# Where the normed state lies in SBUF: 32 KB of matmul operands move to a pool of their own, at another address modulo 512 bytes

## The chip, the core and the metric

The kernel runs on one core of a Trainium2 chip. TensorE (PE, with PEld for its weight loads), VectorE (DVE), ScalarE (ACT), GpSimd (POOL) and the DMA queue that SyncE (SP) issues work side by side and meet at semaphores. The metric is the device time of one execution in microseconds (us), lower is better, as the median of several runs.

## The reference, cut to what matters

The program is a two-layer diffusion backbone over 256 latent tokens and 256 context tokens of width 1024, everything in float32. Layer 0 mixes tokens by a grouped 2-D Fourier transform, layer 1 by retention. Each layer puts a half-step SwiGLU feed-forward block (FFN, inner width 2816) before and after its mixer.

```python
def _modnorm(h, g, shift, scale):
    return _rmsnorm(h, g) * (1.0 + scale) + shift

def _ffn_half(h, g, shift, scale, gate, w_in, w_out):
    a, b = jnp.split(_modnorm(h, g, shift, scale) @ w_in, 2, axis=-1)
    return h + 0.5 * gate * ((jax.nn.silu(a) * b) @ w_out)
...
for i in range(DEPTH):
    h = _ffn_half(h, norm_g[i, 0], m[:, 0], m[:, 1], m[:, 2], ffn_w_in[i, 0], ffn_w_out[i, 0])
    u = _modnorm(h, norm_g[i, 1], m[:, 3], m[:, 4])
    ...
    h = h + m[:, 5] * y
    h = _ffn_half(h, norm_g[i, 2], m[:, 6], m[:, 7], m[:, 8], ffn_w_in[i, 1], ffn_w_out[i, 1])
```

The normed state u is what every first matrix of a block multiplies: `w_in` of the FFN, the queries, keys and gates of retention, and the channel transform of the Fourier mixer.

## The kernel before

The state is held transposed: 128 features on the partitions, tokens along the free dimension, latent tokens in columns 0 to 255 and context tokens in 256 to 511. A product in float32 is made of three float32r matmuls: each operand is split into a high part (tag `h`, or pool `hip`) and a low part (tag `l`, or `lop`), and `mm3` (lines 132 to 135) issues high times high (L133), high weights times low state (L134) and low weights times high state (L135), each with a weight load of its own of 128x128.

`new_u` (line 272) hands out the normed state: 16 tiles `uh0`, `ul0` ... `uh7`, `ul7` of 128 x 512 float32r, 2048 bytes of each partition. It is called seven times, and since the tags repeat and the pool has one buffer for a tag, all seven users share the same 16 places. In a trace all of these tiles are called `u`.

Weights come in through `unit` (line 114): 512 KB loads into `raw` (pool `rawp`, 7 buffers), a copy to `hi` by ACT (L121) and a difference to `lo` by DVE (L122), pools of 3 buffers of 2048 columns each. Every 128x128 block of weights begins a multiple of 512 bytes from the start of its tile, since 128 float32 are 512 bytes; so does every block of columns taken out of `u` or of `g`. `gp` (21 buffers of 128 x 512, named `g`) holds the SwiGLU products, the Fourier results, queries, keys and so on, and `bigp` (8 buffers of 128 x 1024, named `big`) the context stream and, in layer 1, the mixed tokens.

The first half of an FFN is done in 22 units of 128 inner features. A unit has 2 accumulations (gate and value) over 8 blocks k, so 2 x 8 x 3 = 48 matmuls, `mm<-u,hi` and `mm<-u,lo`, 512 columns wide where both streams run (FFNs 1, 2 and 3, by `ffn(0,0)`, `ffn(0,1)`, `ffn(1,0)`) and 256 wide in the last FFN, `ffn(1,1)`, which runs latent tokens alone. In FFNs 2 and 3 the first two units are done by halves of 256 columns. The second half is `mm<-g,hi` and `mm<-g,lo`. The 22 units go in chunks of 8, 8 and 6, each followed by its share of the second half. In retention `queries` (256 wide) and `keys` (512 wide) stream u past the weights; `gates` loads u as the weights and streams the 512 columns of a `hi` or `lo` tile (`mm<-hi,u`), and `outputs` does the same with `g` as weights (`mm<-hi,g`). In the last FFN, two units read not u but `pre`, which lies in `big` tiles as three blocks of 258 columns in a row (line 783).

While the FFNs of layer 0 and the first of layer 1 run, DVE also computes the modulation vectors of later layers (L173), a `mod_piece` for most units.

Pools lie one after the other in SBUF in the order in which they are made, and within `cst` (one buffer for each tile) the tiles lie in the order in which they are first asked for. Line 578 asks for a tile that nothing uses:

```python
    cst.tile([P, 8], F32, name="pad")
```

Of the kernel before, what the change touches and what calls it, by code (L numbers as in the profile page):

```python
# [11 lines left out]
F32 = mybir.dt.float32  # L12
F32R = mybir.dt.float32r
# [4 lines left out]
P = 128  # L18
# [3 lines left out]
NT = 512  # L22
FT = 22
CHUNKS = ((0, 8), (8, 16), (16, 22))
HEADS = 4
EPS = 1e-6
HALVES = ((0, 256), (256, 512))
S_C, S_B, S_G, S_FG, S_LG, S_W = 0, 16, 160, 208, 216, 224

# [2 lines left out]
def hybrid_kernel(ctx: ExitStack, tc: tile.TileContext, small, conds, xT, wm0, wm, w_in, w_out,  # L32
# [4 lines left out]
    def pool(name, bufs, **kw):  # L37
        return ctx.enter_context(tc.tile_pool(name=name, bufs=bufs, **kw))

    cst = pool("cst", 1)  # L40
    rawp = pool("rawp", 7)
    hip = pool("hip", 3)
    lop = pool("lop", 3)
# [8 lines left out]
    def nm(s):  # L52
        uid[0] += 1
        return f"{s}_{uid[0]}"

    def gtile(dt):
        return gp.tile([P, NT], dt, tag="g", name=nm("g"))
# [23 lines left out]
    hl = [cst.tile([P, 2, NL], F32, name=f"hl{j}") for j in range(4)]  # L81
    hc = [big(F32).rearrange("p (k n) -> p k n", k=4) for _ in range(2)]

    def H(k, v):
        return hl[k // 2][:, k % 2, :] if v == 0 else hc[k // 4][:, k % 4, :]
# [42 lines left out]
    def split(hi, lo, src):  # L128
        A.activation(hi, src, AF.Copy)  # L129
        V.tensor_tensor(lo, src, hi.bitcast(F32), op=ALU.subtract)  # L130
# [14 lines left out]
    def mod_slice(j):  # L145

        raw = [load(wm0[j, :, a:a + 1024]) for a in (0, 1024)]
        ps = stat()
        for kk in range(2):
            for g in range(4):  # L150
                kt = 2 * g + kk
                T.matmul(ps[32 * g:32 * g + 32, :256], c32[:, kt, :], raw[kt // 4][:, kt % 4 * 256:(kt % 4 + 1) * 256],  # L152
                         start=(kk == 0), stop=(kk == 1), tile_position=(0, 32 * g))
        if j == 0:
            keep_warm(raw[1], 8)
        rows = wk.tile([P, 256], F32, tag="ut", name=nm("mr"), bufs=4)
        A.activation(rows, ps[:, :256], AF.Copy)
        pc = stat()
        for c in range(2):
            T.matmul(pc[:, 2 * c:2 * c + 2], rows[:, c * P:(c + 1) * P], sel, start=True, stop=True)  # L160
            V.tensor_tensor(mods[0, c][:, :, j], pc[:, 2 * c:2 * c + 2], bias[:, 0, c, j:j + 1].to_broadcast([P, 2]),
                            op=ALU.add)
# [22 lines left out]
    def scaled_gain(l, j, c, vs):  # L185
        g = cst.tile([P, 2, KT], F32, name=f"gain{l}_{j}")
        gn = sm[:, S_G + (3 * l + j) * 8:S_G + (3 * l + j) * 8 + 8]
        for v in range(vs):
            V.scalar_tensor_tensor(g[:, v, :], mods[l, c][:, v, :], 1.0, gn, op0=ALU.add, op1=ALU.mult)
        return g  # L190
# [54 lines left out]
    def rstd_cols(*vs):  # L245
# [7 lines left out]
        ms = wk.tile([P, 4], F32, tag="ms", name=nm("ms"))[:, :n]  # L253
        V.tensor_scalar(ms, ps[:, 0:n], EPS, None, op0=ALU.add)
        y = wk.tile([P, 4], F32, tag="rs", name=nm("rs"))[:, :n]
# [3 lines left out]
    def rstd(*vs, meanwhile=None):  # L259
        n = 2 * len(vs)  # L260
        y = rstd_cols(*vs)
        if meanwhile is not None:
            meanwhile()
        for v in vs:
            normed[v] = newest[0]
        pr = stat()
        for i in range(n):
            T.matmul(pr[:, i * P:(i + 1) * P], y[:, i:i + 1].to_broadcast([P, P]), ident,  # L268
                     start=True, stop=True)
        return pr  # L270

    def new_u():
        return [tuple(cst.tile([P, NT], F32R, tag=f"u{x}{k}", name=nm("u")) for x in "hl")
                for k in range(KT)]

    def modnorm(u, v, gain, shift, pr=None, ks=range(KT), whole=None):
        a, b = HALVES[v]
        if pr is None:
            pr = rstd(v)
        for k in ks:  # L280
            t = wk.tile([P, NL], F32, tag="ut", name=nm("ut"), bufs=4)
            V.scalar_tensor_tensor(t, H(k, v), gain[:, v, k:k + 1], pr[:, :NL],  # L282
                                   op0=ALU.mult, op1=ALU.mult)
            s = shift[:, v, k:k + 1]
            A.activation(u[k][0][:, a:b], t, AF.Identity, bias=s)  # L285
            V.scalar_tensor_tensor(u[k][1][:, a:b], t, s, u[k][0][:, a:b].bitcast(F32),  # L286
                                   op0=ALU.add, op1=ALU.subtract)
            if whole is not None:
                if v == 0:
                    whole.append(gtile(F32))  # L290
                A.activation(whole[k][:, a:b], t, AF.Identity, bias=s)
# [32 lines left out]
    def ffn(l, i, u, gate_c, streams, done, first=None, after=None):  # L324
        parts = [(HALVES[v], (v,)) for v in streams]
        full = ((0, 256 * len(streams)), tuple(streams))
        for ci, (f0, f1) in enumerate(CHUNKS):
# [27 lines left out]
            def out_tiles(dp, w, part):  # L355
                (a, b), vs = part
                for dd in range(2):
# [5 lines left out]
                    for v in vs:  # L363
                        x, y = HALVES[v]
                        V.scalar_tensor_tensor(H(d, v), ps[:, x - a:y - a], gate[:, v, d:d + 1],  # L365
# [26 lines left out]
    def norm_into(l, j, c_shift, c_scale, vs, whole=None):  # L392
        u = new_u()
        st = {}

        def go(v):
            if not st:
                st["g"] = scaled_gain(l, j, c_scale, vs)
            modnorm(u, v, st["g"], mods[l, c_shift], whole=whole)

        return u, go


    def first(g, u):
# [8 lines left out]
        V.tensor_copy(pb, rstd(0, 1, meanwhile=lambda: mod_slice(0)))  # L413
        pr = [pb[:, a:b] for a, b in HALVES]

# [25 lines left out]


    u = new_u()
    u2 = new_u()
    g2 = []
    cos_c = cst.tile([P, P], F32, name="cos_c")
    sh2 = cst.tile([P, 2, KT], F32, name="sh2")

    def state2(d, v):
        if not g2:  # L450
# [6 lines left out]
            g2.append(scaled_gain(0, 1, 4, 2))  # L457
        a, b = HALVES[v]
        gn = g2[0][:, v, d:d + 1]
# [36 lines left out]
    def tokens(v, k):  # L496
# [7 lines left out]
        V.tensor_tensor(pf[:, 0:1], pf[:, 0:1], sh2[:, v, k:k + 1], op=ALU.add)  # L504
        a, b = HALVES[v]
        split(fr[k][0][:, a:b], fr[k][1][:, a:b], pf[:, :NL])
# [68 lines left out]
        V.tensor_scalar(blg, lg, 256.0, None, op0=ALU.mult)  # L575


    cst.tile([P, 8], F32, name="pad")
    diff = gtile(F32)
    nc.gpsimd.iota(diff.rearrange("p (i n) -> p i n", i=2), pattern=[[-P, 2], [1, NL]], base=0,  # L580
                   channel_multiplier=-1, allow_small_or_imprecise_dtypes=True)
# [112 lines left out]
    def outputs(hd, mx, sg):  # L694
# [11 lines left out]
        for n in range(2):  # L706
# [5 lines left out]
            ve = wk.tile([P, 1], F32, tag="ve", name=nm("ve"))  # L712
            V.tensor_scalar(ve, mv[:, 1:2], EPS, None, op0=ALU.add)
            y = wk.tile([P, 1], F32, tag="gy", name=nm("gy"))
# [164 lines left out]
def build(arrays):  # L879
    import concourse.bacc as bacc  # L880

    nc = bacc.Bacc("TRN2", target_bir_lowering=False, num_devices=1)
    args = [nc.dram_tensor(f"in_{n}", a.shape, F32, kind="ExternalInput").ap() for n, a in arrays]
    args.append(nc.dram_tensor("out_x", (P, KT, NL), F32, kind="ExternalOutput").ap())
    with tile.TileContext(nc) as tc:
        hybrid_kernel(tc, *args)
    return nc
# [10 lines left out]
```

## Time and profile before

| | |
|---|---|
| median of 3 runs | 1707.25 us (1707.1 to 1707.93) |
| the profiled execution | 1707.28 us |
| span of its instructions | 1705.5 us |
| PE busy | 1684.2 us, 99% of the span, 9368 matmuls |
| DVE, ACT busy | 1115.4 us (65%), 600.1 us (35%) |
| DMA | 152 GB/s mean |
| granted TensorE clock, mean | 0.996 |

The span runs from the first instruction to the last; the execution's own time has 1.8 us more around it. Matmuls are pipelined: one that takes 390 ns from its start to its end is followed by the next some 230 ns later, so what a matmul costs is the spacing of starts, not its duration. Spacing is read as the time between the first and the last start of a stretch, divided by the number of steps between them.

### The profile page before, as it was taken

The numbers are of one execution on the slowest core, as the hardware profiler recorded it, in microseconds if no ns is written. First come the engines' busy times: TensorE is split into PE (matmuls) and PEld (weight loads), VectorE is DVE, ScalarE is ACT, GpSimd is POOL, SyncE is SP. The second block draws the span as 40 slices with busy tenths as digits, with TensorE's granted clock in tenths as the row PEclk, the third lists the DMA queues.
The fourth block names the chain that finished last, engine by engine and source line by source line (L and its number), as shares of the span: only waits on it lengthen the run. The fifth ranks groups of instructions, "written<-read, shape, count | busy, mean of one in ns | idle before, by whom it ended". The sixth has DMA issues, their size and how long they took to land.

```text
span 1705.5 us, 23555 instructions
## 1 busy us (share of the span) xinstructions
PE 1684.2 (99%) x9368; PEld 1451.8 (85%) x9368; DVE 1115.4 (65%) x2015; ACT 600.1 (35%) x918; POOL 1.3 (0%) x7
## 2 busy tenths in 40 slices
PE   8999999999999999999999999999999999999997
PEld 5788888889998888888898888888988998899997
DVE  5886677578567845855776545544796767685554
ACT  4331222235333222212342223222574444463443
POOL 0000000000000000000000000000000000000000
PEclk9999999999999999999999999999999999999999
DMA  9665555342115633644325544544233333345551
GB/s 328 234 220 173 173 176 191 138 140 87 68 57 182 194 137 133 201 142 136 136 100 168 177 149 142 188 140 148 102 121 136 116 132 124 128 152 197 190 164 48
DMA packets 73262, 258.74 MB, mean 152 GB/s; under 512 B 8128, under 2 KB 8512, under 8 KB 73152
## 3 DMA queue, kind: packets, MB, share of 16 engines
q1 hardware_dynamic: 73152, 257.24, 44.5%
q8 instruction: 73, 1.20, 0.3%
q14 instruction: 37, 0.30, 0.1%
HBM read 256.16 MB, written 1.05 MB: 151 GB/s over the span
## 4 chain that ended last, share of the span: by engine, by line
PE 95%; DVE 3%; issue 1%; ACT 1%; DMA 0%; SPq 0%; DVEq 0%; ACTq 0%
PE mm L134 31%; PE mm L133 31%; PE mm L135 31%; DVE lo L122 1%; PE st L152 1%; PE st L252 0%; DMA big<-in_xT 0%; ACT hi L121 0%; PE st L268 0%; DVE rb L216 0%; DVE g L494 0%; DVE g L130 0%; PE st L103 0%; DVE g L717 0%; DVE bs L709 0%
## 5 line engine op out<-in xcount | busy, mean ns | idle before, releaser
L121 ACT ACTIVATE hi<-raw 128x1024 fp32r<-128x1024 f32 x346 | 345.5, 1031 | 667.6 <-PE mm L134 477.0
L134 PE MATMUL mm<-u,hi 128*128 128x512 f32 (+1 forms) x1568 | 561.4, 359 | 0.0
L133 PE MATMUL mm<-u,hi 128*128 128x512 f32 (+1 forms) x1568 | 560.2, 359 | 1.2 <-ACT u L285 1.2
L135 PE MATMUL mm<-u,lo 128*128 128x512 f32 (+1 forms) x1568 | 560.6, 359 | 0.0
L122 DVE TENSOR_TENSOR lo<-raw,hi 128x1024 fp32r<-128x1024 f32 x346 | 406.2, 1195 | 57.7 <-ACT hi L121 53.7
L133 PEld LDWEIGHTS mm<-u,hi 128*128 128x128 f32 x1568 | 294.3, 188 | 50.5 <-ACT u L285 2.3
L134 PEld LDWEIGHTS mm<-u,hi 128*128 128x128 f32 x1568 | 294.7, 188 | 48.1 <-DVE u L286 0.6
L134 PE MATMUL mm<-g,hi 128*128 128x256 f32 (+1 forms) x1000 | 335.0, 335 | 0.5 <-DVE g L130 0.4
L133 PE MATMUL mm<-g,hi 128*128 128x256 f32 (+1 forms) x1000 | 334.8, 336 | 0.8 <-ACT g L129 0.8
L135 PEld LDWEIGHTS mm<-u,lo 128*128 128x128 f32 x1568 | 294.4, 188 | 48.2 <-issue 1.2
L135 PE MATMUL mm<-g,lo 128*128 128x256 f32 (+1 forms) x1000 | 334.5, 335 | 0.0
L173 DVE CUSTOM_DVE_ANT_0 prod<-raw,big,sm 128x1024 bf16<-128x1024 f32 x224 | 275.7, 1282 | 0.0
L303 DVE TENSOR_TENSOR sil<-sil,mm 128x512 f32<-128x512 f32 (+1 forms) x90 | 54.3, 605 | 261.0 <-PE mm L135 251.2
L134 PEld LDWEIGHTS mm<-g,hi 128*128 128x128 f32 x1000 | 189.8, 190 | 20.6 <-DVE g L130 1.4
L133 PEld LDWEIGHTS mm<-g,hi 128*128 128x128 f32 x1000 | 189.3, 190 | 20.2 <-ACT g L129 1.0
L135 PEld LDWEIGHTS mm<-g,lo 128*128 128x128 f32 x1000 | 189.8, 190 | 19.2
L365 DVE SCALAR_TENSOR_TENSOR hl<-mm,gate,hl 128x256 f32<-128x256 f32 x96 | 46.4, 483 | 147.4 <-PE mm L135 147.1
L302 ACT ACTIVATE sil<-mm 128x512 f32<-128x512 f32 (+1 forms) x90 | 47.7, 531 | 215.6 <-PE mm L135 215.6
L130 DVE TENSOR_TENSOR g<-sil,g 128x512 fp32r<-128x512 f32 (+1 forms) x92 | 55.2, 599 | 3.2 <-ACT g L129 3.2
L129 ACT ACTIVATE g<-sil 128x512 fp32r<-128x512 f32 (+1 forms) x92 | 50.3, 547 | 8.2 <-DVE sil L303 8.2
L285 ACT ACTIVATE u<-ut,mod 128x256 fp32r<-128x256 f32 x72 | 33.1, 499 | 41.4 <-DVE ut L282 41.4
L135 PE MATMUL mm<-hi,g 128*128 128x256 f32 (+1 forms) x128 | 43.2, 338 | 0.4 <-DVE g L494 0.2
(174 smaller groups left out, 1211.5 us busy)
## 6 DMA issues: line engine op xcount, KB each, us to landing
raw<-in_w_in SPq DMA_DIRECT2D x176, 512.0 KB, 4.5
raw<-in_wm SPq DMA_DIRECT2D x144, 512.0 KB, 4.7
raw<-in_w_out SPq DMA_DIRECT2D x80, 512.0 KB, 4.3
raw<-in_wvg SPq DMA_DIRECT2D x32, 512.0 KB, 4.3
raw<-in_wqk SPq DMA_DIRECT2D x16, 512.0 KB, 4.5
raw<-in_wro SPq DMA_DIRECT2D x16, 512.0 KB, 4.1
raw<-in_w_out SPq DMA_DIRECT2D x16, 256.0 KB, 2.7
raw<-in_wf SPq DMA_DIRECT2D x8, 512.0 KB, 3.8
```

The lines of the kernel that those rows point to most:

```text
L121: A.activation(hi[:, a:b], raw, AF.Copy)
L122: i = V.tensor_tensor(lo[:, a:b], raw, hi[:, a:b].bitcast(F32), op=ALU.subtract).ins
L129: A.activation(hi, src, AF.Copy)
L130: V.tensor_tensor(lo, src, hi.bitcast(F32), op=ALU.subtract)
L133: T.matmul(ps, l[0], r[0], start=first, stop=False)
L134: T.matmul(ps, l[0], r[1], start=False, stop=False)
L135: T.matmul(ps, l[1], r[0], start=False, stop=last)
L173: V.tensor_tensor_reduce(t, raw, crow[v], 1.0, bias[:, l, c, k:k + 1], ALU.mult, ALU.add, mods[l, c][:, v, k:k + 1])
L285: A.activation(u[k][0][:, a:b], t, AF.Identity, bias=s)
L302: i = A.activation(s[:, :n], pab[0][:, :n], AF.Silu).ins
L303: j = V.tensor_tensor(s[:, :n], s[:, :n], pab[1][:, :n], op=ALU.mult).ins
L365: V.scalar_tensor_tensor(H(d, v), ps[:, x - a:y - a], gate[:, v, d:d + 1], H(d, v), op0=ALU.mult, op1=ALU.add)
```

## The change

The tiles of `new_u` come from a pool `up`, made right after `cst`. The tile `pad` keeps its 8 columns, now under a name.

```diff
@@
 EPS = 1e-6
+PAD = 8
 HALVES = ((0, 256), (256, 512))
@@
     cst = pool("cst", 1)
+    up = pool("up", 1)
     rawp = pool("rawp", 7)
@@
     def new_u():
-        return [tuple(cst.tile([P, NT], F32R, tag=f"u{x}{k}", name=nm("u")) for x in "hl")
+        return [tuple(up.tile([P, NT], F32R, tag=f"u{x}{k}", name=nm("u")) for x in "hl")
                 for k in range(KT)]
@@
-    cst.tile([P, 8], F32, name="pad")
+    cst.tile([P, PAD], F32, name="pad")
```

In the built program no instruction is added, removed or moved on any engine, and no wait differs. What differs are byte addresses (of a partition):

| tiles | before | modulo 512 | after | modulo 512 |
|---|---|---|---|---|
| `u`, 16 tiles | 27264 to 60031 | 128 | 29952 to 62719 | 256 |
| small tiles made after u (`cos_c`, `sh2`, `mod`, `gain`, `gate`, `lg`, `dec`, `pad`) | from 60032 | mixed | from 27264, each 32768 lower | as before |
| `raw`, `hi`, `lo`, `g`, `big` | 62720, 91392, 115968, 140544, 183552 | 256 | the same | 256 |
| `hl` (latent state), `ident` | 17984, 17408 | 64, 0 | the same | 64, 0 |

## Rows read from the trace of the kernel before

**Rows 1.** The page's first lines: the span, and busy time and instructions by engine.

```profile
span 1705.5 us, 23555 instructions
PE 1684.2 (99%) x9368; PEld 1451.8 (85%) x9368; DVE 1115.4 (65%) x2015; ACT 600.1 (35%) x918; POOL 1.3 (0%) x7
PEclk9999999999999999999999999999999999999999
```

**Rows 2.** All waits of PE: total us, times, longest (the longest group shown).

```profile
engine line waited for: us in total, times, longest us
PE st L252 <- DVE ss L236: 5.0, 2, 2.8
PE st L268 <- DVE rs L218: 2.3, 1, 2.3
...
PE mm L133 <- ACT u L285: 1.2, 1, 1.2
```

**Rows 3.** Groups of matmuls, shapes apart: xcount | busy us, mean ns of one | idle.

```profile
L135 PE MATMUL mm<-u,lo 128*128 128x512 f32 x1056 | 417.8, 396 | 0.0
L133 PE MATMUL mm<-g,hi 128*128 128x512 f32 x488 | 190.0, 389 | 0.0
L134 PE MATMUL mm<-g,hi 128*128 128x256 f32 x512 | 145.1, 284 | 0.5 <-DVE g L130 0.4
L135 PE MATMUL mm<-u,lo 128*128 128x256 f32 x512 | 142.9, 282 | 0.0
L134 PE MATMUL mm<-lo,u 128*128 128x512 f32 x64 | 25.3, 395 | 0.0
L134 PE MATMUL mm<-lo,g 128*128 128x512 f32 x64 | 24.9, 390 | 0.0
L135 PE MATMUL mm<-hi,u 128*128 128x256 f32 x32 | 9.1, 283 | 0.0
```

**Rows 4.** L133 in five stretches: duration ns min/median/max, first and last start us.

```profile
L133 PE MATMUL mm<-u,hi x108: 392/395/398, 174.9 to 249.8; 128*128 128x512 f32 x108
L133 PE MATMUL mm<-g,hi x57: 389/389/389, 261.6 to 299.7; 128*128 128x512 f32 x57
L133 PE MATMUL mm<-u,hi x72: 390/393/404, 74.2 to 123.7; 128*128 128x512 f32 x72
L133 PE MATMUL mm<-u,hi x92: 390/393/404, 884.2 to 947.7; 128*128 128x512 f32 x92
L133 PE MATMUL mm<-g,hi x18: 389/389/389, 445.0 to 456.5; 128*128 128x512 f32 x18
```

**Rows 5.** Timeline of PE, first and last of 128 matmuls on g.

```profile
start us, us, engine line op out<-in xcount [idle before <-releaser]
1557.72 0.28 PE L134 MATMUL mm<-g,hi 128*128 128x256 f32 x1
...
1572.96 0.28 PE L135 MATMUL mm<-g,lo 128*128 128x256 f32 x1
```

**Rows 6.** Timeline of PE, first and last of 157 matmuls on u.

```profile
1599.78 0.28 PE L133 MATMUL mm<-u,hi 128*128 128x256 f32 x1
...
1618.29 0.28 PE L133 MATMUL mm<-u,hi 128*128 128x256 f32 x1
```

**Rows 7.** Matmuls on `big` in the last FFN, block k = 6, then block k = 7.

```profile
L134 PE MATMUL mm<-big,hi x3: 283/283/283, 1512.8 to 1513.5; 128*128 128x258 f32 x3
L135 PE MATMUL mm<-big,lo x3: 283/283/283, 1512.9 to 1513.6; 128*128 128x258 f32 x3
L134 PE MATMUL mm<-big,hi x4: 279/280/286, 1513.9 to 1514.9; 128*128 128x258 f32 x4
L135 PE MATMUL mm<-big,lo x4: 278/280/281, 1514.0 to 1515.0; 128*128 128x258 f32 x4
```

**Rows 8.** Stretches: us, busy time (instructions) by engine, PEclk, DMA share, GB/s.

```profile
0.00:60.00 60.00, 52.33 (x338) 37.58 (x339) 35.80 (x99) 23.90 (x40) 0.70 (x6) 0.94 0.84 300
60.00:125.00 65.00, 65.00 (x281) 52.73 (x280) 57.90 (x86) 23.64 (x31) 0.00 (x0) 1.00 0.68 227
175.00:250.00 75.00, 75.00 (x323) 60.35 (x322) 50.70 (x75) 21.69 (x28) 0.00 (x0) 1.00 0.52 175
```

**Rows 9.** Groups of the stretch 172 to 250 us.

```profile
L121 ACT ACTIVATE hi<-raw 128x1024 fp32r<-128x1024 f32 x14 | 14.1, 1053 | 33.2 <-PE mm L134 33.2
L122 DVE TENSOR_TENSOR lo<-raw,hi 128x1024 fp32r<-128x1024 f32 x15 | 17.7, 1222 | 0.8 <-ACT hi L121 0.3
```

**Rows 10.** Timeline of PEld and of PE near 200 us.

```profile
200.12 0.19 PEld L134 LDWEIGHTS mm<-u,hi 128*128 128x128 f32 x1
200.11 0.40 PE L133 MATMUL mm<-u,hi 128*128 128x512 f32 x1
```

**Rows 11.** Groups of weight loads, shapes apart.

```profile
L135 PEld LDWEIGHTS mm<-u,lo 128*128 128x128 f32 x1568 | 294.4, 188 | 48.2 <-issue 1.2
L134 PEld LDWEIGHTS mm<-g,hi 128*128 128x128 f32 x1000 | 189.8, 190 | 20.6 <-DVE g L130 1.4
L134 PEld LDWEIGHTS mm<-g,big 128*128 128x128 f32 x128 | 24.6, 192 | 0.1
```

## The prediction

> **What bounds the kernel now.** I read the page's head first. [...] The waits of PE come next: the longest group is 5.0 us, and the one that names u is 1.2 us [rows 2]. So the end is set by how densely matmuls follow each other, and only two things can change the time: the spacing of matmuls, or a feed that falls behind and makes PE wait. Since the change moves no instruction, I look at spacing by shape and by operand.
>
> Grouped by shape, matmuls of the same 128x512 shape differ: 396 ns on u, 389 on g [rows 3]. With 256 columns it is the other way round, 282 on u and 284 on g [rows 3]. Durations overlap, so the price has to come from spacing [rows 4]. On u between 174.9 and 249.8 us there are 107 steps of three matmuls: 74.9 / 321 = 233.3 ns. On g between 261.6 and 299.7 us: 38.1 / 168 = 226.8 ns. The difference of 6.5 ns agrees with that of the durations (395 against 389). Two other stretches on u give 49.5 / 213 = 232.4 ns (first FFN, 74 to 124 us) and 63.5 / 273 = 232.6 ns (third FFN, from 884 us) [rows 4]. For 256 columns, 128 matmuls on g take 15.24 us from the first start to the last, 120.0 ns a step [rows 5], and 157 on u take 18.51 us, 118.65 ns a step [rows 6].
>
> Also to be seen: on g each duration is 389, minimum, median and maximum alike, and on u they scatter from 392 to 398 [rows 4]. A steady value marks g, a scattered one u.
>
> **Is it the place that makes the difference?** u lies at 128 modulo 512, everything else that a matmul reads in bulk at 256, weights included. Three comparisons keep other things equal. First, the Fourier mixer's output matmuls (445 to 457 us) have the FFN's shape and loop over 8 blocks, but stream g tiles, and they show the steady 389 [rows 4]: the loop is not the cause. Second, in retention u is the loaded operand and a 256-modulo tile the streamed one, and the group is again slow, 395 against 390 with g loaded [rows 3]: it is not the streaming side of u that counts, but the pair. Third, the last FFN's first two units stream blocks of `big` tiles high in SBUF. Block k = 6 begins at 256 modulo 512, block k = 7 at 264; the first shows 283/283/283, the second 277 to 286 [rows 7], as u does. So the scatter follows the place and not the region of SBUF in which u happens to lie. This last comparison is over a dozen matmuls each, and its mean durations do not price the 512-column case.
>
> A mechanism that fits: the next weight load starts within 10 ns of the matmul ahead of it and runs beside it for 188 ns [rows 10, 11], so both operands are being read at once, and it matters how the two reads fall on SBUF. [...]
>
> **The change part by part.** The pool `up` and the name `PAD` cost nothing by themselves: no instruction, wait or queue entry is added. The small tiles that move down by 32768 bytes are read by ACT and DVE as scalars and keep their place modulo 512; I take them at zero. Writing u at another place is work of ACT and DVE that lies beside PE, except for the 1.2 us of [rows 2]; I take zero for it too, and if these writes changed by a tenth, that would be 0.1 us. What remains is the spacing of the matmuls on u, which after the change have streamed and loaded operands both at 256, as those on g have now.
>
> Term one, 512 columns. There are 3 x 1056 matmuls that stream u and 3 x 64 that load it [rows 3], 3360 in all. By the program 384 of them are in the first eight units of FFN 1, 288 in the last six of FFN 3's first chunk and 384 in retention; for these 1056 I take 232.5 ns (the two slower stretches measured above, and for retention the nearest in duration). The other 2304 are at 233.3. Saved: 2304 x (233.3 - 226.8) = 15.0 us, and 1056 x (232.5 - 226.8) = 6.0 us, together 21.0 us.
>
> Term two, 256 columns. 3 x 512 stream u and 96 load it [rows 3]. At g's spacing they lose 1632 x (120.0 - 118.65) = 2.2 us.
>
> Net: 21.0 - 2.2 = 18.8 us. The profiled execution took 1707.28 us (0.03 above the median of the runs), so the forecast is 1707.3 - 18.8 = **1688.5 us**, with a span of 1686.7 us.
>
> **What could eat it: the feeds.** A unit of the FFN will ask for its weights every 48 x 226.8 = 10.9 us in place of 11.2. In the steady stretch from 175 to 250 us DVE is busy 50.7 of 75 us and the DMA engines 52% [rows 8], and ACT's copies to `hi` sat 33.2 us waiting for PE to release buffers [rows 9]: weights are ready and wait for PE, so a faster PE finds them ready too. The tight place is the first FFN. From 60 to 125 us DVE is busy 57.9 of 65 us; 2.4% less time makes that 91%, still under full. From 0 to 60 us the DMA engines are 84% busy and PE is busy 52.3 us [rows 8], so part of the gain there may become waiting. If all of it did in the first eight units: 384 x 5.7 = 2.2 us less gain. The same again if retention, with its chains of short stages, gave nothing back: 384 x 5.7 = 2.2 us. Both together give 1692.9 us. On the other side, if the 256-column matmuls keep 118.65, the gain is the full 21.0 us: 1686.3.
>
> **The rivals.**
> *No change.* The spacing on u has a cause that stays with u: its region of SBUF, or what ACT and DVE do in the same stretches. [...] Against it: the comparison of blocks 6 and 7 [rows 7], and the steady 389 between 261.6 and 299.7 us while DVE and the loads go on as before [rows 4]. Time: 1707.3 us, or 1709.5 if the 256-column ones alone move to 120.0.
>
> *Slower.* A common place delays every pair a little, which is what the 256-column rows show: 1.35 ns more at 256 on 256 than on 128, and weight loads of 190 to 192 ns beside g against 188 beside u [rows 11]. If that is all that the place does, and the 6.5 ns at 512 columns are due to something else that stays, each of the 3360 matmuls gains 1.35 ns too: 3360 x 1.35 + 2.2 = 6.7 us, 1714.0 us. It decides from the point where the 512-column spacing on u falls by less than 0.65 ns: 3360 x 0.65 ns is 2.2 us and no longer pays for term two. Against it is that the wide matmuls on g are not slower but faster than those on u.
>
> *Half of it.* On u there are at least two lasting patterns, 232.4 and 233.3 ns, for the same addresses [rows 4]: the spacing depends also on how the two reads happen to fall in time. If an aligned u settled in a pattern halfway, the gain of term one halves: 21.0 / 2 - 2.2 = 8.3 us, 1699.0 us. Against it: g shows one value, 389, in each of the stretches read.
>
> *The feed becomes the bound* in the first FFN and retention, as priced above: 1690.7 to 1692.9 us.
>
> **How the numbers follow.** The forecast 0.78; the feed eats a part 0.10; half of it 0.04; no change 0.05; slower 0.03. Runs of this kernel spread by 0.05%, and I count 0.2%, 3.4 us, as what can be told from no change. Faster: 0.78 + 0.10 + 0.04 = 0.92; same 0.05; slower 0.03. The range takes in both bounds of the unknown costs, 1686.3 less the spread of runs and 1692.9: 1685.8 to 1693.0 us. Outside it lie the other three cases, 0.12.
>
> **What the profile after would show.** Right: the groups of 128x512 on u, streamed and loaded, at 389 to 390 ns with minimum, median and maximum equal, and a spacing of 226.8 in all four stretches; 256 columns on u at 283 steady and 120.0 ns apart; the groups on g as before; weight loads beside u at 190 ns or so; PE's waits as now or a few us more between 20 and 70 us; a span of 1686.7 us. Wrong: durations on u still 392 to 398 (no change or slower, told apart by whether the spacing rose), or 389 with the time gone into idle time ahead of PE, which the waits would name. It would also be wrong in size if the aligned spacing on u were not g's.

## The result and the profile after

The changed kernel takes 1689.22 us (median of 4 runs, 1686.90 to 1690.31) against 1707.45 us for the kernel before (4 runs): a ratio of 0.9891, 95% interval 0.9874 to 0.9908, so 1.1% faster. The profiled execution took 1688.18 us. The forecast was 1688.5 us with a span of 1686.7; the span came out at 1686.4.

The head of the page after (span, and busy time and instructions by engine) answers to [rows 1]:

```profile
span 1686.4 us, 23555 instructions
PE 1664.9 (99%) x9368; PEld 1452.3 (86%) x9368; DVE 1115.2 (66%) x2015; ACT 599.9 (36%) x918; POOL 1.3 (0%) x7
```

The span lost 19.1 us and PE's busy time 19.3. PE's time without work was 1705.5 - 1684.2 = 21.3 us and is 1686.4 - 1664.9 = 21.5 us: all of the gain is denser matmuls, and none of it was lost to waiting. The groups of matmuls by shape (xcount | busy us, mean ns | idle) show where; L135 to L137 are L133 to L135 of before, two lines further down:

```profile
L137 PE MATMUL mm<-u,lo 128*128 128x512 f32 x1056 | 411.7, 390 | 0.0
L135 PE MATMUL mm<-g,hi 128*128 128x512 f32 x488 | 190.0, 389 | 0.0
L137 PE MATMUL mm<-u,lo 128*128 128x256 f32 x512 | 143.5, 283 | 0.0
L136 PE MATMUL mm<-lo,u 128*128 128x512 f32 x64 | 24.9, 390 | 0.0
```

Against [rows 3] the 512-column matmuls on u fell from 396 to 390 ns, streamed or loaded (395 to 390), those on g stayed at 389, and the 256-column ones on u rose from 282 to 283. L135 in four stretches (duration ns min/median/max, first and last start us) answers to [rows 4], and the last row to [rows 6]:

```profile
L135 PE MATMUL mm<-u,hi x116: 389/389/389, 171.7 to 249.9; 128*128 128x512 f32 x116
L135 PE MATMUL mm<-u,hi x70: 389/389/389, 73.8 to 120.7; 128*128 128x512 f32 x70
L135 PE MATMUL mm<-u,hi x83: 389/389/389, 874.1 to 929.8; 128*128 128x512 f32 x83
L135 PE MATMUL mm<-u,hi x68: 283/283/283, 1569.8 to 1594.0; 128*128 128x256 f32 x68
```

Each duration on u is now the steady value of g. The spacing is 78.2 / 345 = 226.7 ns in the steady stretch (233.3 before), 46.9 / 207 = 226.6 and 55.7 / 246 = 226.4 in the two that were at 232.4 and 232.6, and 24.2 / 201 = 120.4 ns at 256 columns. First and last starts are given to 0.1 us, which is worth 0.2 to 0.5 ns here. The timeline gives starts to 0.01 us, and for the 256-column stretch it shows 24.12 / 201 = 120.0 ns (118.65 before):

```profile
1569.83 0.28 PE L135 MATMUL mm<-u,hi 128*128 128x256 f32 x1
...
1593.95 0.28 PE L135 MATMUL mm<-u,hi 128*128 128x256 f32 x1
```

The feeds kept up. The stretch of the first FFN with the most DVE work (us, busy time by engine, clock, DMA share, GB/s), beside [rows 8]:

```profile
60.00:125.00 65.00, 65.00 (x288) 53.85 (x287) 58.94 (x88) 24.52 (x32) 0.00 (x0) 1.00 0.69 231
```

PE has no idle time in it, starts 288 matmuls where it started 281, and DVE is at 58.94 / 65 = 91%, as worked out. The longest waits of PE are those of [rows 2]:

```profile
PE st L254 <- DVE ss L238: 5.1, 2, 3.2
PE st L270 <- DVE rs L220: 2.3, 1, 2.3
...
PE mm L135 <- ACT u L287: 1.2, 1, 1.2
```

### The profile page after: what moved, and what is told of

Its sections match the earlier page's. It is cut to its first block, busy times and chain, and to the rows that moved or that the text cites. A ratio compares the mean times of both kernels' runs of the same rounds, so it can differ in the third digit from the quotient of the medians.

```text
span 1686.4 us, 23555 instructions
## 1 busy us (share of the span) xinstructions
PE 1664.9 (99%) x9368; PEld 1452.3 (86%) x9368; DVE 1115.2 (66%) x2015; ACT 599.9 (36%) x918; POOL 1.3 (0%) x7
## 4 chain that ended last, share of the span: by engine, by line
PE 94%; DVE 3%; issue 1%; ACT 1%; DMA 0%; SPq 0%; DVEq 0%; ACTq 0%
PE mm L136 31%; PE mm L135 31%; PE mm L137 31%; DVE lo L124 1%; PE st L154 1%; PE st L254 0%; DMA big<-in_xT 0%; ACT hi L123 0%; PE st L270 0%; DVE rb L218 0%; DVE g L496 0%; DVE g L132 0%; DVE u L288 0%; DVE ut L284 0%; PE st L105 0%
## 5 line engine op out<-in xcount | busy, mean ns | idle before, releaser
L135 PE MATMUL mm<-u,hi 128*128 128x512 f32 (+1 forms) x1568 | 554.9, 355 | 1.2 <-ACT u L287 1.2
L137 PE MATMUL mm<-u,lo 128*128 128x512 f32 (+1 forms) x1568 | 555.2, 355 | 0.0
L135 PE MATMUL mm<-g,hi 128*128 128x256 f32 (+1 forms) x1000 | 334.7, 336 | 0.8 <-ACT g L131 0.8
L137 PE MATMUL mm<-g,lo 128*128 128x256 f32 (+1 forms) x1000 | 334.5, 335 | 0.0
L135 PEld LDWEIGHTS mm<-u,hi 128*128 128x128 f32 x1568 | 295.9, 189 | 44.4 <-ACT u L287 2.3
L137 PEld LDWEIGHTS mm<-u,lo 128*128 128x128 f32 x1568 | 295.9, 189 | 41.8 <-issue 1.2
L135 PEld LDWEIGHTS mm<-g,hi 128*128 128x128 f32 x1000 | 189.3, 190 | 20.2 <-ACT g L131 1.0
L137 PEld LDWEIGHTS mm<-g,lo 128*128 128x128 f32 x1000 | 189.8, 190 | 19.1
L137 PE MATMUL mm<-hi,g 128*128 128x256 f32 (+1 forms) x128 | 43.3, 338 | 0.3 <-DVE g L496 0.2
```

Source lines behind the costliest of these rows:

```text
L135: T.matmul(ps, l[0], r[0], start=first, stop=False)
L137: T.matmul(ps, l[1], r[0], start=False, stop=last)
```

## The experiments

All start from the changed kernel. To move a pool by a few dozen bytes without moving what lies behind it, small tiles of `cst` (64 bytes each for a `mod`, 32 for `pad` or `lg`) are taken from a pool made further on. "Distance" is the address of the streamed operand less that of the loaded one, modulo 256 (why 256 is seen in the third run). For each run a few rows are shown, most from the source view of the line that was L133 in the kernel before, with durations min/median/max and the first and last start.

**u back at its old place, in its own pool.**

```diff
+LATE = [(1, 8), (1, 7)]
...
     up = pool("up", 1)
+    late = pool("late", 1)
...
-        mods[l, c] = cst.tile([P, 2, KT], F32, name=f"mod{l}_{c}")
+        p = late if (l, c) in LATE else cst
+        mods[l, c] = p.tile([P, 2, KT], F32, name=f"mod{l}_{c}")
```

> The pool of its own stays, but u begins 128 bytes lower, at 128 modulo 512, its place of before; hi, lo, g and big stay at 256. Pair theory (the distance modulo 512 between what is streamed and what is loaded beside it sets the spacing): durations on u at 512 columns 392 to 398 and scattered, spacing 232 to 233.3 ns, 256 columns 118.7 ns, a time of 1707.3 us as before the change (1706 to 1709). Rival (the pool of its own, or the region from 29 KB up, made the gain): 389 steady, 226.7 ns, 1688 to 1690 us.

Measured: 1707.91 us, ratio to the kernel before 1.0001 (0.9992 to 1.0010).

```profile
L137 PE MATMUL mm<-u,hi x104: 392/395/398, 175.2 to 247.3; 128*128 128x512 f32 x104
```

72.1 / 309 = 233.3 ns, with the old scatter. A shift of 128 bytes takes the whole gain away; the pool of its own and the new order of tiles are worth nothing.

**Everything at 128.** The pool `late` with the same two tiles is made after `bigp` in place of after `up`, so that u, raw, hi, lo, g and big all move down by 128 bytes.

> u, raw, hi, lo, g and big all begin 128 bytes lower than in the changed kernel, so all at 128 modulo 512: distance zero, another place. Pair theory: as the changed kernel, 389 steady on u and g, 226.7 ns and 120.0 ns, 1688 to 1690 us. Rival (256 itself is the good place for a bulk operand): u and g both scatter at 232 to 233.3 ns; 3360 matmuls on u and some 1656 on g of 512 columns at 6.3 ns more and about 3800 of 256 columns at 1.2 ns less, so 1707 + 10 - 3 = 1714 us.

Measured: 1689.15 us, ratio 0.9890 (0.9875 to 0.9904).

```profile
L137 PE MATMUL mm<-u,hi x108: 389/389/389, 175.0 to 247.8; 128*128 128x512 f32 x108
```

72.8 / 321 = 226.8 ns. u lies at 128 modulo 512 as it did before the change, and is fast: the place in itself made no difference (226.7 at 256 in the changed kernel), the distance did (233.3 in the run above).

**u half a period away.** As the first run, with four `mod` tiles in `late`: u at 0 modulo 512, the weights at 256.

> u begins 256 bytes lower than in the changed kernel, at 0 modulo 512, half a period away from hi and lo. Pair theory with a period of 512: not distance zero, so off the steady 389; if any distance costs the same as 128, 233 ns and 1707 us; if the cost grows with distance up to half a period, more, up to 240 ns and 1730 us. Rival (the period is 256, not 512): 389 steady, 226.7 ns, 1688 to 1690 us. Rival (a distance exists that is better than zero): under 226 ns at 512 columns, under 1685 us.

Measured: 1689.25 us, ratio 0.9892 (0.9876 to 0.9909).

```profile
L137 PE MATMUL mm<-u,hi x108: 389/389/389, 175.1 to 247.9; 128*128 128x512 f32 x108
```

(247.9 - 175.1) / 321 = 226.8 ns again. 256 bytes apart was as good as none, so the period is 256 bytes and not the 512 of the change's description.

**128 bytes on the other side.** Six `mod` tiles: u at 384 modulo 512.

> u begins 384 bytes lower than in the changed kernel, at 384 modulo 512, 128 bytes on the other side of hi and lo. Pair theory with a cost that is the same on both sides: as before the change, 232 to 233.3 ns at 512 columns, 118.7 at 256, 1707 us. What speaks for it: where u was loaded and a 256-modulo tile streamed, the distance had the other sign, and the durations were 395 too. Rival (the sign matters, since the loaded operand starts a little after the streamed one): another spacing, either near 227 ns and 1689 us or above 235 ns and 1714 us.

Measured: 1707.63 us, ratio 1.0000 (0.9991 to 1.0009).

```profile
L137 PE MATMUL mm<-u,hi x105: 392/392/398, 175.2 to 248.0; 128*128 128x512 f32 x105
```

72.8 / 312 = 233.3 ns, as a period of 256 says: 128 up is 128 down.

**64 and 32 bytes below.** One `mod` tile in `late`; then the tile `pad` alone in it.

> u begins 64 bytes lower than in the changed kernel (192 modulo 512; hi and lo at 256). The runs so far: distance 0 and 256 give 226.8 ns and 120.0, distance 128 on either side 233.1 and 118.8. Theory A (only a distance of a multiple of 256 is good, every other costs the same): 233 ns at 512 columns, 118.8 at 256, span 1706. Theory B (the cost grows with the distance up to 128): about 230 ns, span near 1696. Theory C (64 or 128 bytes is the grain of a finer pattern): 226.8 again, or under it, span 1686 or less.

Measured: 1701.79 us in one run, span 1700.0. The second row is of the last FFN.

```profile
L137 PE MATMUL mm<-u,hi x104: 394/394/394, 175.3 to 247.4; 128*128 128x512 f32 x104
L137 PE MATMUL mm<-u,hi x102: 276/276/276, 1579.8 to 1614.2; 128*128 128x256 f32 x102
```

At 512 columns the spacing is 72.1 / 309 = 233.3 ns, so the "every other costs the same" of theory A holds there, though each duration shown is 394: a slow place need not scatter. At 256 columns it fails: 34.4 / 303 = 113.5 ns, 6.5 less than at distance 0, where A said 118.8. That is why this kernel is quicker than the kernel before, by 5.4 us beside the median of its runs on the same chip (1707.16).

> u begins 32 bytes lower than in the changed kernel (224 modulo 512; hi and lo at 256). Theory A (every distance but a multiple of 256 costs the same): 233 ns, span 1706. Theory B (the cost grows with the distance up to 128): about 228 ns, span near 1691. What speaks for A: block 7 of the last FFN's first units, 8 bytes off the place, scattered at once from 277 to 286 where block 6 stood at 283.

Measured: 1707.74 us in one run, span 1705.9.

```profile
L136 PE MATMUL mm<-u,hi x105: 395/396/396, 174.8 to 247.6; 128*128 128x512 f32 x105
L136 PE MATMUL mm<-u,hi x97: 277/280/285, 1584.7 to 1618.8; 128*128 128x256 f32 x97
```

72.8 / 312 = 233.3 ns and 34.1 / 288 = 118.4 ns: as theory A, and the gain at 256 columns is gone.

**The weights moved away from g.** The pool `late` with two `mod` tiles is made after `lop`: raw, hi, lo and u go down by 128 bytes together, g and big stay.

> raw, hi, lo and u all begin 128 bytes lower than in the changed kernel (128 modulo 512), g and big stay at 256. So u and the weights have distance zero and g and the weights 128. Pair theory: u stays at 389 steady and 226.8 ns, and it is now g that scatters at 392 to 398: 1464 matmuls of 512 columns that stream g and 192 that load it at some 6.3 ns more, 10.4 us, and 1728 of 256 columns at 1.2 ns less, 2.1 us, so 1689.2 + 8.3 = 1697.5 us. Rival (something about the u stages, not the pair, is what the place cures): g stays at 226.8, 1689 us. Rival (128 modulo 512 is a bad place for u in itself): u back at 233, 1707 us or more.

Measured: 1697.21 us, ratio 0.9940 (0.9925 to 0.9955).

```profile
L137 PE MATMUL mm<-u,hi x108: 389/389/389, 175.0 to 247.8; 128*128 128x512 f32 x108
L137 PE MATMUL mm<-g,hi x50: 392/395/398, 262.2 to 296.5; 128*128 128x512 f32 x50
```

The roles are exchanged: u is steady at 72.8 / 321 = 226.8 ns, and g scatters at 34.3 / 147 = 233.3. The time is within 0.3 us of the sum. Nothing about the u stages was special; it was the pair.

**128 bytes for the narrow matmuls only.** In the last FFN, which uses 256 of the 512 columns of its tiles, u and g take other columns.

```diff
-    u6 = new_u()
+    u6 = [tuple(x[:, 32:32 + NL] for x in pair) for pair in new_u()]
...
             g = {f: (gtile(F32R), gtile(F32R)) for f in range(f0, f1)}
+            if len(streams) == 1:
+                g = {f: tuple(x[:, 32:32 + NL] for x in pair) for f, pair in g.items()}
```

> As the changed kernel, but in the last FFN, whose matmuls are 256 columns wide, u and g use columns 32 to 287 of their tiles of 512 in place of 0 to 255, so a distance of 128 bytes to the weights where that is the better one. Pair theory: 960 matmuls on u and 528 on g go from 120.0 to 118.8 ns, 1.8 us, so 1687.4 us, everything else as in the changed kernel. Rival (the 1.2 ns are lost to something else in that stage, such as the weights' loads): 1689.2 us. A time under the changed kernel's by 0.1% is near what the runs can tell, so the spacing in the last FFN decides.

Measured: 1688.18 us, ratio to the kernel before 0.9887 (0.9871 to 0.9904).

```profile
L135 PE MATMUL mm<-u,hi x83: 279/281/285, 1569.8 to 1599.0; 128*128 128x256 f32 x83
```

29.2 / 246 = 118.7 ns, the spacing that was expected. The time does not tell it from the changed kernel: the difference is 1.0 us, and the runs of the changed kernel alone spread by 3.4. Inside the two traces it can be read: from the first 258-column matmul of the last FFN to the end of the span this kernel takes 1686.5 - 1483.7 = 202.8 us and the changed one 1686.4 - 1482.3 = 204.1, so 1.3 us of the 1.8 expected are seen.

**The other distances.** By two pools of late tiles, one after `up` and one after `lop`, u and g get distances of their own: u 96 below and g 64 above the weights (a `mod` and `pad` behind u, a `mod` behind `lop`); then u 160 below, which is 96 above, and g 32 above (two `mod` and `pad` behind u, `lg` behind `lop`).

> Two distances in one kernel: u lies 96 bytes below hi and lo modulo 256, g 64 bytes above them. Seen so far at 512 columns: 226.7 ns at distance 0, 233.3 at 128, 64 below and 32 below; at 256 columns: 120.0 at 0, 118.7 at 128, 118.3 at 32 below, 113.3 at 64 below. Steps theory (the spacing takes steps of 6.67 ns, 226.7 and 233.3, 113.3 and 120.0, and the sign of the distance does not matter): u 233.3 at 512, g 233.3 at 512 and 113.3 at 256; 3360 x 6.6 + 1656 x 6.6 - 1728 x 6.7 - 1632 x 1.2 is 20 us over the changed kernel, a span near 1706. Rival (the sign matters): g at 512 columns keeps 226.7 or falls to 220, and a span of 1695 or less.

Measured: 1710.39 us in one run, span 1708.6.

```profile
L137 PE MATMUL mm<-u,hi x104: 392/397/400, 175.2 to 247.6; 128*128 128x512 f32 x104
L137 PE MATMUL mm<-g,hi x52: 388/388/388, 261.6 to 296.7; 128*128 128x512 f32 x52
L137 PE MATMUL mm<-u,hi x108: 277/280/282, 1584.8 to 1622.5; 128*128 128x256 f32 x108
...
L137 PE MATMUL mm<-g,hi x46: 396/397/398, 713.4 to 744.9; 128*128 128x512 f32 x46
```

u is at 72.4 / 309 = 234.3 ns, and at 37.7 / 321 = 117.4 with 256 columns. g is at 35.1 / 153 = 229.4 in one stretch (34.79 / 152 = 228.9 by the timeline, to 0.01 us) and at 31.5 / 135 = 233.3 in another of the same execution, with the same addresses. Neither side of the expectation was right on g: 64 above is not 64 below, but no stretch is under the 226.7 of distance 0. At 256 columns on g the mean duration of this group is 280, against 285 for the same group of the changed kernel:

```profile
L137 PE MATMUL mm<-g,hi 128*128 128x256 f32 x512 | 142.5, 280 | 0.7 <-ACT g L133 0.7
```

That mean mixes at least two patterns:

```profile
L137 PE MATMUL mm<-g,hi x27: 276/276/276, 464.0 to 472.9; 128*128 128x256 f32 x27
L137 PE MATMUL mm<-g,hi x51: 279/279/279, 1558.0 to 1575.7; 128*128 128x256 f32 x51
```

By the timeline the first is at 8.84 / 78 = 113.3 ns and the second, in the last FFN, at 17.55 / 149 = 117.8.

> Two distances in one kernel: u lies 160 bytes below hi and lo modulo 256, which is 96 above, and g 32 bytes above. If the sign does not matter: u at 512 columns near 233 and at 256 columns as at 96 below; g at 512 columns 233.3 and at 256 columns 118.3, as u at 32 below: 3360 x 6.5 + 1656 x 6.6 - 3360 x 1.5 is 28 us over the changed kernel, a span near 1714. Rival (above and below differ): a spacing at 512 columns under 226.7 or at 256 columns under 118 in one of the two.

Measured: 1716.39 us in one run, span 1714.6.

```profile
L137 PE MATMUL mm<-u,hi x105: 399/399/399, 175.1 to 247.9; 128*128 128x512 f32 x105
L137 PE MATMUL mm<-g,hi x51: 393/396/397, 261.9 to 296.9; 128*128 128x512 f32 x51
L137 PE MATMUL mm<-u,hi x121: 278/278/283, 1584.8 to 1628.0; 128*128 128x256 f32 x121
L137 PE MATMUL mm<-g,hi x53: 277/280/280, 1563.7 to 1581.9; 128*128 128x256 f32 x53
```

u 72.8 / 312 = 233.3 ns, g 35.0 / 150 = 233.3, u at 256 columns 43.2 / 360 = 120.0 and g at 256 columns 18.2 / 156 = 116.7. The span is within 1 us of the sum of the side on which the sign does not matter, but the 256-column terms of that sum are not what was measured: 96 above stands at 120.0 where 96 below stood at 117.4, and 32 above at 116.7 where 32 below stood at 118.4. The rival, a spacing under 118 at 256 columns, came true on g. Nothing is under 226.7 at 512 columns here either; this is the slowest kernel of the study.

**The best distance tried, for each width.** As the kernel with 128 bytes for the narrow matmuls, with columns 48 to 303, 192 bytes up, which is 64 below modulo 256: distance 0 where matmuls are 512 wide, 64 below in the last FFN.

> As the changed kernel, but in the last FFN, 256 columns wide, u and g use columns 48 to 303 of their tiles, 192 bytes above the weights modulo 256, which is 64 below. 512-column matmuls stay at distance 0. If the 113.3 ns seen at 64 below belong to the distance: 960 matmuls on u and 528 on g go from 120.0 to 113.3 ns, 9.9 us, 1679.3 us, and everything else as in the changed kernel. Rival (another chain of that stage ends last once the matmuls are quicker, such as the loads, 0.56 of the DMA engines there, or ACT and DVE): idle time of PE in the last 200 us takes part of it, 1682 to 1689 us. Rival (columns 48 on are not what 64 bytes of the tile's start are): 120.0 or 118.7 ns, 1687 to 1689 us.

Measured: 1679.57 us (5 runs, 1679.10 to 1681.72), ratio to the kernel before 0.9838 (0.9825 to 0.9851).

```profile
L135 PE MATMUL mm<-u,hi x95: 276/276/276, 1561.9 to 1593.9; 128*128 128x256 f32 x95
L135 PE MATMUL mm<-g,hi x23: 276/276/279, 1594.9 to 1602.9; 128*128 128x256 f32 x23
```

32.0 / 282 = 113.5 ns, and PE's waits took nothing of it back: PE is without work for 1677.8 - 1657.5 = 20.3 us, where it was 21.5. The medians of this kernel and the changed one differ by 1689.22 - 1679.57 = 9.7 us, with 9.9 expected, and without an instruction more. That 192 above does here what 64 below did for u also speaks for the period of 256.

## Why the prediction was right

*What bounds the kernel.* Right: PE was busy for 99% of the span before and after, and the change of the span is the change of PE's busy time, 19.1 against 19.3 us.

*The pair, not the operand, the region or the stage.* Right, and shown from both sides: moving u alone by 128 bytes takes the gain away (233.3 ns, 1707.91 us), moving all together leaves it (226.8 ns, 1689.15 us), moving the weights away from g hands the loss to g (233.3 ns on g, 226.8 on u). That both operands are being read at once, and that the two reads get in each other's way, was only argued: [rows 10] and [rows 11] show a weight load of 188 ns that lies beside a matmul of 396. The runs show that the distance between the streamed and the loaded operand decides; they do not show which two accesses meet.

*The copies of the weights, a rival that the runs' times leave open.* `raw`, `hi` and `lo` moved together in every run, so the partner of the streamed tile could also be the weights being written beside PE, and not those being loaded. The kernel with the weights moved away from g can tell: in its retention g streams past `hi` at 128 and past `big` at 0, with copies to `hi` and `lo` going on (the last two rows are of 1317 to 1327 us).

```profile
L138 PE MATMUL mm<-g,big x32: 280/283/283, 1316.9 to 1328.1; 128*128 128x256 f32 x32
L138 PE MATMUL mm<-g,hi x16: 274/281/285, 1313.0 to 1329.8; 128*128 128x256 f32 x16
L125 ACT ACTIVATE hi<-raw 128x1024 fp32r<-128x1024 f32 x2 | 2.0, 1052 | 2.3 <-issue 2.3
L126 DVE TENSOR_TENSOR lo<-raw,hi 128x1024 fp32r<-128x1024 f32 x3 | 3.6, 1212 | 0.0
```

With `big` loaded g stands at 283, the value of distance 0, and with `hi` loaded it scatters around 281. So in this stretch, at 256 columns, it is the loaded operand that counts.

*The rival of no change.* If the spacing on u had a cause that stays with u, the changed kernel would have stayed at 1707 us. The measurement decides: it took 1689.22 us, and the spacing on u at 512 columns fell from 233.3 to 226.7 ns in the steady stretch, with u in the same stages and 2688 bytes higher.

*Term one*, 21.0 us at 512 columns. In the mean durations it is (396 - 390) x 3168 + (395 - 390) x 192 = 20.0 us, with means rounded to 1 ns; by the spacing of the three stretches (226.7, and 226.5 for the two that were at 232.4 and 232.6) 2304 x 6.6 + 1056 x 6.0 = 21.5 us. The term lies between. The prediction calls those two stretches the slower ones; they are the quicker ones, and its sum uses their figures rightly.

*Term two*, a loss of 2.2 us at 256 columns. The mean durations rose by about 1 ns, 1.6 us for 1632 matmuls; the spacing rose from 118.65 to 120.0 in the stretch read, 2.2 us. Sign and size hold.

*Net* 18.8 us forecast, 19.1 us in the spans.

*The feeds.* The 91% of DVE came out as worked out, and the 2.2 us set aside for the first eight units were not needed: in 74 to 121 us the spacing is 226.6 ns with every duration at 389. The other 2.2 us, for retention, were hardly needed: the groups that load u stand at 390, and in `keys`, which stream it, the slowest group (of 1200 to 1500 us) fell by 5 ns. Before, then after:

```profile
L135 PE MATMUL mm<-u,lo 128*128 128x512 f32 x64 | 25.5, 399 | 0.0
L137 PE MATMUL mm<-u,lo 128*128 128x512 f32 x64 | 25.2, 394 | 0.0
```

*The half-gain rival.* It was right to fear lasting patterns, but in the stretches read on a pair at distance 0 none but 226.4 to 226.8 was seen. At 64 above, 228.9 and 233.3 stand in one execution. That a pattern comes from how the two reads fall in time was the author's guess; no run shows it.

*The clock.* Every slice of [rows 1] shows 0.9 of full speed or more, but that is a mean over some 43 us: in the kernel before the granted clock was 0.63 from 10 to 15 us and 0.68 from 15 to 20. Nothing in the sum hangs on it.

Three things were not seen ahead. The period is 256 bytes, so that 256 bytes apart (226.8 ns), wrong by the change's description, is as good as zero (226.7). And 256 columns have their best place elsewhere: the prediction knew two distances and took the loss at 256 columns as the price of alignment, while 64 below gains 6.5 ns there. And a steady duration marks neither g nor a good place: at 64 below u stood at 394/394/394 and lost as much at 512 columns as at 128 (233.3 ns each).

## What to carry to other kernels

Where PE is the bound and each matmul has a weight load of its own, compare the durations and the spacing of equal shapes by operand. Here a difference, 396 ns on u against 389 on g, was the sign that the place of the streamed tile relative to the weights cost time, 6.5 ns a matmul. A scatter was such a sign too, but the steady 394 at 64 below was as slow (233.3 ns), so the spacing decides. Moving u to another pool added no instruction (23555 before and after). In this kernel, float32r with 128x128 weights, the best distance of those tried was 0 modulo 256 bytes for 512 columns (226.7 ns) and, in the last FFN, 64 below for 256 columns (113.5 ns). It has to be measured for each shape: here it was neither "aligned" nor the same for both. Two small `mod` tiles put into a pool of their own moved the time of the changed kernel from 1689.22 to 1707.91 us, 1.1%, through this alone, so check the addresses before crediting any other edit.

## What the runs showed of the hardware that was not expected

Spacing in ns per matmul by distance (streamed less loaded, modulo 256 bytes), from the stretches above; distance 0 at 256 columns from [rows 5]. Two values are two lasting patterns of one distance. Where one stands it is that of the stretch read; other stretches can hold another:

| distance | 512 columns | 256 columns |
|---|---|---|
| 0 | 226.7 | 120.0 |
| 32 above | 233.3 | 116.7 |
| 64 above | 228.9 or 233.3 | 113.3 or 117.8 |
| 96 above | 233.3 | 120.0 |
| 128 | 233.3 | 118.7 |
| 96 below | 234.3 | 117.4 |
| 64 below | 233.3 | 113.5 or 117.7 |
| 32 below | 233.3 | 118.4 |

The second value at 64 below is of FFN 2 in the kernel with u 64 bytes below (10.95 / 93 by the timeline):

```profile
L137 PE MATMUL mm<-u,hi x32: 281/281/281, 496.7 to 507.7; 128*128 128x256 f32 x32
```

226.7 is twice 113.4, and 233.3 and 120.0 lie 6.6 and 6.5 ns above these two, but 116.7 to 118.7, 228.9 and 234.3 are no such steps. The trace's starts, in whole ns, show that a value of the table is the mean of a pattern that repeats: 229, 238, 229, 237 ns at 128 bytes in the kernel before, but 233 or 234 each time at 64 below. Why a distance settles in one pattern or another, and why the two widths prefer different distances, stays open.

Part of the spread between the runs of one kernel goes with the mean granted clock: the changed kernel took 1686.90, 1688.18, 1690.25 and 1690.31 us at 0.997, 0.996, 0.995 and 0.995. In the profiled execution of the changed kernel the clock is short of full within the first 30 us, in which PE is busy for 22.2: 0.65 from 10 to 15 us and 0.67 from 15 to 20, and 1.00 in the other four windows of 5 us; from 30 to 1686 us the mean is 1.00. In windows of the kernel with 128 bytes for the narrow matmuls, whose mean was 0.994:

```profile
15.00:20.00 5.00, 5.00 (x37) 4.12 (x29) 3.02 (x11) 2.38 (x3) 0.00 (x0) 0.66 0.97 397
20.00:25.00 5.00, 3.69 (x31) 2.32 (x32) 4.96 (x11) 3.99 (x6) 0.00 (x0) 1.00 0.92 325
25.00:30.00 5.00, 5.00 (x18) 3.54 (x17) 4.70 (x9) 2.10 (x4) 0.00 (x0) 0.66 1.03 374
```

Here the granted clock falls a second time, to 0.66 of full in the mean of a window, after one in which PE was busy 3.69 of 5 us. The changed kernel has the same 3.69 us there and no second fall:

```profile
20.00:25.00 5.00, 3.69 (x32) 2.31 (x32) 4.96 (x11) 3.75 (x6) 0.00 (x0) 1.00 0.92 321
25.00:30.00 5.00, 5.00 (x28) 3.31 (x26) 4.94 (x9) 2.34 (x4) 0.00 (x0) 1.00 1.03 381
```

What makes the difference is not shown. In the four runs above two thousandths of the mean clock go with 3.4 us. The runs of the kernel before that were made beside the experiments show less, from a mean of 1709.0 us at 0.994 (4 runs) to 1706.5 at 0.997 (5 runs), and the kernel with 128 bytes for the narrow matmuls took 1687.93 to 1688.45 us at 0.994 in all four runs. So the clock is not the whole of the spread, which is larger than the smallest effect measured here.
